# Layer 1's FFN down projection by seven products on 2x2 blocks for 16 of its 22 tiles

## The chip, the cores and the metric

The kernel runs on one core of one Trainium2 chip. TensorE (PE) multiplies, VectorE (DVE) and ScalarE (ACT) do elementwise work, GpSimd (POOL) and SyncE (SP) issue DMAs here. The metric is the device time of one execution in microseconds (us), as the median of several runs. Times of stages come from one profiled execution, counted from its span's start.

## The reference

A two-layer encoder trunk on 1024 tokens of width 1024. Every layer ends with a SwiGLU FFN, whose output is gated and added to the residual stream; a final RMS norm follows layer 1. What the change touches is the product with `w2` in layer 1:

```python
def swiglu(h, w1, w3, w2):
    return (jax.nn.silu(h @ w1) * (h @ w3)) @ w2
...
        h = rms_norm(x, norm_ffn[layer]) * (1.0 + scale_f) + shift_f
        x = x + gate_f * swiglu(h, ffn_w1[layer], ffn_w3[layer], ffn_w2[layer])
    return rms_norm(x, final_norm)
```

`w1` and `w3` are 1024 x 2816, `w2` is 2816 x 1024.

## The kernel before

The activations lie transposed: a tile holds 128 features in the partitions and 1024 tokens, used as two halves of 512 (`HALVES`). The hidden width 2816 makes 22 such tiles, `acts[0]` to `acts[21]`; the model width makes 8 row tiles, `xT[0]` to `xT[7]`.

Each float32 operand of a matmul is split into a high part, rounded to the type fp32r by an ACT copy, and a low part, the rest, by a DVE subtract (`split_into`, L262). A product is then three passes: high times high, high times low, low times high. PE gets one matmul of 128x128 by 128x512 for each pass, each with a weight load of its own.

The FFN (`ffn`, L589) has two stages. In the up products, `w1` and `w3` are taken in 11 pairs of tiles; a pair is two units (one of each weight). From the second pair on, a unit is done by seven products of blocks instead of eight (Winograd's form of Strassen's scheme): the weight blocks and their sums are the left operands, made one by one by `prep` (ACT and DVE) and three products ahead; the activations and their sums are the right operands, `B["11"]`, `B["t1"]` and so on, made once. A product has 12 matmuls (L626 to L628). After the two units of a pair, `done(p, s)` stores the two finished tiles in DRAM (`sp_f`, by POOL), except for the last four, which stay.

The down projection reads the tiles back in groups of 4, 4, 4, 4, 3 and 3, splits them, and adds each group's product with `w2` to the residual `xT` by one DVE operation for each half (`matvec_add`, L795, matmuls at L303, additions at L813). The last group goes one half at a time (`matvec_halves`, L823), so that the final norm (`final`, `normed`, L485) of the first half runs beside the products of the second.

SBUF is cut into equal buffers that the code calls pages, `repage(nf, nr)`: nf of float32 and nr of fp32r, each handed out first in, first out. PSUM has eight banks. The order of instructions on each engine is set when the kernel is built: a scheduler reorders what the code emits. At run time each engine works its queue in order, and an instruction that waits holds back all behind it.

Of the kernel before, what the change touches and what calls it, by code (L numbers as in the profile page):

```python
# [10 lines left out]
F32 = mybir.dt.float32  # L11
# [10 lines left out]
P = 128  # L22
# [54 lines left out]
class Kern:  # L77
# [407 lines left out]
    def normed(self, xT, steps, use, lag, keep=None):  # L485

        nc = self.nc
        acc, sq = self.page(), [self.page() for _ in range(2)]  # L490
        todo, r = deque(), []

        def some(c):
            for _ in range(min(c, len(todo))):
                use(*todo.popleft())

        def half(n):
            r.append(self.rstd(acc, n))
            todo.extend((n, m, r[n]) for m in range(KT))

        for n, m in steps:
            cs = HALVES[n]
            s = sq[m % 2][:, cs] if m else acc[:, cs]
            nc.scalar.activation(out=s, in_=xT[m][:, cs], func=AF.Square)
            if m:
                nc.vector.tensor_tensor(out=acc[:, cs], in0=acc[:, cs], in1=s, op=ALU.add)
            if keep is not None:
                nc.sync.dma_start(out=keep[m][:, cs], in_=xT[m][:, cs])
            if n == 1:
                if m == lag:  # L510
                    half(0)
                elif m > lag:
                    some(2)
        self.free(sq)
        half(1)
        some(2 * KT)
        self.free(acc)
        self.fbank(r)
# [70 lines left out]
    def ffn(self, xT, before, layer, up=iter(()), down=iter(()), low=None):  # L589
# [86 lines left out]
        acts = {}  # L676

        def done(p, s):
            for a in range(2):
                j = 2 * p + a  # L680
# [5 lines left out]

        done(0, s)
        B["t3"] = B.pop("12")
# [27 lines left out]
        for u in range(2, len(units)):  # L716
# [13 lines left out]
            for name in ("11", "t2", "21", "t1", "t3", "t4", "22"):  # L730
# [5 lines left out]
                if u == len(units) - 1:  # L736
                    self.free(B[name])
                if name == "11":
                    nc.scalar.copy(q, ps)
# [22 lines left out]
            if w is w3:  # L762
                done(p, s)
            run(some(up, 3))
        run(up)


# [24 lines left out]
        at, n = groups[-1]  # L792
        return xT, self.matvec_halves(xT, w2[at * P : (at + n) * P, :], ys, layer, 5, low)

    def matvec_add(self, xT, w, ys, layer, part, g=0, keep=None, low=False):  # L795
# [1308 lines left out]
def build(ctx, tc, ins, out):  # L2104
# [73 lines left out]
    ys = K.hyena(hw_in, h, lambda y: project(xd, y, hw_out[0], 1))  # L2178
    K.repage(13, 33)
    xT = [K.unspill(d) for d in xd]  # L2180
# [86 lines left out]
```

## Time and profile before

| | |
|---|---|
| median of 3 runs | 3352.37 us (3352.03 to 3354.47) |
| profiled execution's own time | 3352.85 us |
| its span | 3351.1 us |
| layer 1's up products | up to some 3083 us |
| layer 1's down projection | 3083 to 3331 us |
| final norm of the second half, transposes, output | 3331 to 3351 us |

Rows of the timeline and of groups read: line, engine, operation, tiles written and read (p is any SBUF buffer, bk a PSUM bank), partitions by elements, count, busy time and mean, and then the idle time just before with what ended it ("<-"). Windows give, for each stretch, the busy time of PE, PEld (weight loads), DVE, ACT and POOL with counts, the clock granted to PE, the mean busy share of the 16 DMA engines, and GB/s.

### The profile page before, as it was taken

Reading aid. Unit: us, or ns where it says so; the run is one execution under the profiler, and the core shown is the slowest. Engines: PE = TensorE matmul, PEld = TensorE weight load, DVE = VectorE, ACT = ScalarE, POOL = GpSimd, SP = SyncE. Lnnn points to the kernel's source line nnn. Section 1 sums busy time; section 2 is a strip of 40 time slices with the busy share of each in tenths; the row PEclk is TensorE's granted clock in tenths of the full one; section 3 lists DMA queues with packets and bytes.
Section 4 is the critical chain, followed back from the end, with each engine's and each line's share of the span. In section 5 each row is a group of like instructions: output and inputs, shape, how many; then the busy total and the mean of one; then the engine's idle time right before and its main releaser. Section 6 shows DMA issues by size and latency. Waiting matters only on the chain.

```text
span 3351.1 us, 50857 instructions
## 1 busy us (share of the span) xinstructions
PE 3143.0 (94%) x20195; PEld 2552.3 (76%) x20195; DVE 2331.4 (70%) x3755; ACT 1231.4 (37%) x2144; POOL 196.9 (6%) x443
## 2 busy tenths in 40 slices
PE   6999999988989989999999999988977899999998
PEld 4787766766767878888888887877866788888887
DVE  6465565665766897887877666698998686666545
ACT  4632365555546442533333333221220443333211
POOL 2000000000001110000001210000000000000000
PEclk8999999989989999999999999999988999999999
DMA  8654433333323235344448983332446322234311
GB/s 281 219 179 142 142 96 71 74 85 72 100 65 113 85 134 201 101 145 145 157 132 291 353 296 133 107 113 89 145 169 226 132 82 76 76 107 144 118 48 51
DMA packets 331375, 460.23 MB, mean 137 GB/s; under 512 B 101816, under 2 KB 233745, under 8 KB 331136
## 3 DMA queue, kind: packets, MB, share of 16 engines
q1 hardware_dynamic: 292576, 322.04, 31.2%
q0 software_dynamic: 38384, 134.86, 11.4%
q8 instruction: 159, 2.61, 0.3%
q14 instruction: 80, 0.66, 0.1%
q10 hardware_dynamic: 176, 0.07, 0.0%
HBM read 312.71 MB, written 141.56 MB: 136 GB/s over the span
## 4 chain that ended last, share of the span: by engine, by line
PE 73%; DVE 11%; DMA 8%; ACT 3%; issue 3%; SPq 1%; POOL 0%; DVEq 0%; ACTq 0%; POOLq 0%
PE bk L303 27%; PE bk L626 8%; PE bk L628 8%; PE bk L627 8%; PE bk L1840 2%; DVE p L1722 2%; PE bk L1374 2%; PE bk L1310 2%; PE bk L996 1%; PE bk L975 1%; PE bk L1859 1%; DMA p<-in_mix_w_in_dram 1%; DVE p L264 1%; PE bk L952 1%; DMA p<-in_ada_w_dram 1%
## 5 line engine op out<-in xcount | busy, mean ns | idle before, releaser
L303 PE MATMUL bk<-p,p 128*128 128x512 f32 x5136 | 1228.0, 398 | 73.0 <-ACT p L263 43.2
L303 PEld LDWEIGHTS bk<-p,p 128*128 128x128 f32 x5136 | 974.7, 191 | 289.2 <-ACT p L263 45.6
L263 ACT ACTIVATE p<-p 128x512 fp32r<-128x512 f32 (+3 forms) x542 | 403.1, 759 | 937.5 <-PE bk L627 292.3
L264 DVE TENSOR_TENSOR p<-p,p 128x512 fp32r<-128x512 f32 (+3 forms) x542 | 452.1, 850 | 237.4 <-ACT p L263 195.6
L627 PE MATMUL bk<-p,p 128*128 128x512 f32 x1248 | 485.5, 389 | 3.8 <-DVE p L264 3.8
L626 PE MATMUL bk<-p,p 128*128 128x512 f32 x1248 | 485.0, 390 | 0.0
L628 PE MATMUL bk<-p,p 128*128 128x512 f32 x1248 | 484.7, 389 | 0.2 <-DVE p L264 0.2
L627 PEld LDWEIGHTS bk<-p,p 128*128 128x128 f32 x1248 | 234.3, 188 | 53.1 <-DVE p L264 4.7
L628 PEld LDWEIGHTS bk<-p,p 128*128 128x128 f32 x1248 | 234.3, 188 | 49.2 <-DVE p L264 0.6
L626 PEld LDWEIGHTS bk<-p,p 128*128 128x128 f32 x1248 | 234.3, 188 | 48.1
L813 DVE SCALAR_TENSOR_TENSOR p<-bk,mod,p 128x512 f32<-128x512 f32 x192 | 135.0, 746 | 84.7 <-PE bk L303 83.9
L1722 DVE TENSOR_TENSOR p<-p 128x512 f32<-128x512 f32 x240 | 152.9, 692 | 0.4
L455 DVE SCALAR_TENSOR_TENSOR p<-p,cond,p 128x512 f32<-128x512 f32 x140 | 104.6, 749 | 47.7 <-DMA p<-in_ada_w_dram 45.8
L1840 PE MATMUL bk<-p,p 128*128 128x256 f32 x512 | 125.7, 393 | 6.5 <-DVE p L1761 2.3
L956 DVE TENSOR_REDUCE mx<-bk 128x1 f32<-128x512 f32 x128 | 86.6, 686 | 39.1 <-PE bk L953 37.7
L1840 PEld LDWEIGHTS bk<-p,p 128*128 128x128 f32 x512 | 95.1, 193 | 22.4 <-DVE p L1761 3.1
L1068 ACT COPY p<-bk 128x512 f32<-128x512 f32 (+1 forms) x80 | 43.4, 589 | 177.7 <-PE bk L303 70.6
L960 ACT ACTIVATE p<-bk,mx 128x512 f32<-128x512 f32 x128 | 87.2, 688 | 46.4 <-DVE mx L957 42.5
L976 ACT COPY p<-bk 128x512 f32<-128x512 f32 x128 | 73.5, 588 | 77.3 <-PE bk L975 74.6
L1374 PE MATMUL bk<-p,p 64*64 64x64 f32 x2048 | 86.3, 232 | 13.0 <-DMA p<-o 10.4
L1374 PEld LDWEIGHTS bk<-p,p 64*64 64x64 f32 x2048 | 75.4, 144 | 29.2 <-issue 13.5
L975 PE MATMUL bk<-k_ident,p 128*128 128x128 f32 x512 | 88.6, 302 | 8.2 <-ACT p L976 4.7
(408 smaller groups left out, 4134.7 us busy)
## 6 DMA issues: line engine op xcount, KB each, us to landing
p<-in_ffn_w_dram SPq DMA_DIRECT2D x120, 512.0 KB, 4.7
p<-in_ada_w_dram SPq DMA_DIRECT2D x96, 512.0 KB, 4.5
sp_f<-p POOLq DMA_DIRECT2D x36, 512.0 KB, 5.5
p<-sp_f POOLq DMA_DIRECT2D x36, 512.0 KB, 5.8
hs<-p POOLq DMA_DIRECT2D x32, 512.0 KB, 3.1
p<-hs SPq DMA_DIRECT2D x32, 512.0 KB, 4.5
p<-sp_r SPq DMA_DIRECT2D x24, 512.0 KB, 6.3
p<-sp_x SPq DMA_DIRECT2D x24, 512.0 KB, 4.4
```

Source lines behind the costliest of these rows:

```text
L263: self.nc.scalar.activation(out=hi, in_=src, func=AF.Copy)
L264: self.nc.vector.tensor_tensor(out=lo, in0=src, in1=hi.bitcast(F32), op=ALU.subtract)
L303: nc.tensor.matmul(ps[n], a, b[:, HALVES[n]], start=s, stop=e)
L455: nc.vector.scalar_tensor_tensor(out=acc, in0=wt[:, i], scalar=self.cond[:, k : k + 1], in1=acc, op0=ALU.mult, op1=ALU.add)
L626: nc.tensor.matmul(ps, op[:, 0, k], mh, start=start and k == 0, stop=False)
L627: nc.tensor.matmul(ps, op[:, 0, k], ml, start=False, stop=False)
L628: nc.tensor.matmul(ps, op[:, 1, k], mh, start=False, stop=stop and k == 3)
L813: nc.vector.scalar_tensor_tensor(out=xs, in0=ps[n], scalar=self.modc(layer, part, m), in1=xs, op0=ALU.mult, op1=ALU.add)
L975: nc.tensor.transpose(pt[:, j], pr[:, k * P : (k + 1) * P], self.ident)
L1374: nc.tensor.matmul(pt[H[p], pr], lhs(e, pr, p), rhs[H[p], 8 * e + pr], start=True, stop=True)
L1722: tt = lambda o, a, b, op: nc.vector.tensor_tensor(out=o, in0=a, in1=b, op=op)
L1840: nc.tensor.matmul(ps[j][:, ri], F[2 * d + t2 // 4][:, t2 % 4, 128 * ri : 128 * ri + 128], tp[:, j, d], start=d == 0, stop=d == 1)
```

## The change

For the pairs 0 to 7 of layer 1, the two finished tiles are no longer stored as they are. They are taken as the four blocks of a right operand of seven products: two tiles by two halves. `done` becomes a generator with seven steps; one step is emitted after each product of the next pair. A step makes one right operand: ACT writes its high part (`hi`) and the negated high part (`neg`), POOL stores `hi` in DRAM, SP stores the float32 value, and a POOL DMA with `accum_op=ALU.add` adds `neg` to that in DRAM, so the low part is made there. Four of the steps make the next sum in place by a DVE subtract.

The down projection of layer 1 is a new function, `ffn_down`. Six tiles (18 to 21, 16, 17) go as before. The other sixteen go in two groups of eight: in a group, for each of four blocks of rows (c) there are seven products, each over four k's of 128. The left operands are blocks of `w2` and their sums (`lefts`), the right ones are read back by POOL (`rights`), two names ahead. What a product gives is added to up to four blocks of `xT`. For layer 0 `done` does what it did, one product later. The fp32r buffers of this stage go from 33 to 35, and `normed` counts the tiles of each half itself, since they now come in another order.

```diff
--- before.py
+++ after.py
...
         for n, m in steps:
             cs = HALVES[n]
-            s = sq[m % 2][:, cs] if m else acc[:, cs]
+            i = seen[n]
+            seen[n] += 1
+            s = sq[i % 2][:, cs] if i else acc[:, cs]
             nc.scalar.activation(out=s, in_=xT[m][:, cs], func=AF.Square)
-            if m:
+            if i:
...
-                if m == lag:
+                if i == lag:
                     half(0)
-                elif m > lag:
+                elif i > lag:
...
+        yd = {}
         def done(p, s):
+            if layer and p < 8:
+                b11, b12, b21, b22 = (s[b][:, HALVES[n]] for b in range(2) for n in range(2))
+                for name, src, out, x, y in (
+                    ("11", b11, None, None, None),
+                    ("22", b22, None, None, None),
+                    ("21", b21, b11, b12, b11),
+                    ("t1", b11, b12, b22, b12),
+                    ("t3", b12, b22, b22, b11),
+                    ("t2", b22, b21, b21, b22),
+                    ("t4", b21, None, None, None),
+                ):
+                    d, dl = yd[p, name] = [self.dp.tile([P, 512], dt, tag=f"yd{p}{name}{i}", name=f"yd{p}{name}{i}") for i, dt in enumerate((F32R, F32))]
+                    op = self.page((P, 2, 512), F32R)
+                    hi, neg = op[:, 0], op[:, 1]
+                    nc.scalar.activation(out=hi, in_=src, func=AF.Copy)
+                    nc.scalar.activation(out=neg, in_=hi.bitcast(F32), func=AF.Copy, scale=-1.0)
+                    nc.gpsimd.dma_start(out=d, in_=hi)
+                    nc.sync.dma_start(out=dl, in_=src)
+                    nc.gpsimd.dma_start(out=dl, in_=neg.bitcast(F32), accum_op=ALU.add)
+                    self.free(op)
+                    if out is not None:
+                        tt(out=out, in0=x, in1=y, op=S)
+                    yield
+                self.free(s)
+                return
...
-        done(0, s)
+        side = done(0, s)
...
+                run(some(side, 1))
...
             if w is w3:
-                done(p, s)
+                run(side)
+                side = done(p, s)
             run(some(up, 3))
+        run(side)
         run(up)
+        if layer:
+            return self.ffn_down(xd, acts, yd, w2)
...
+    def ffn_down(self, xd, acts, yd, w2):
...
+        self.repage(25, 23)
+        ys = [self.split(acts[j] if j > 17 else self.unspill(acts[j], nc.gpsimd)) for j in (18, 19, 20, 21, 16, 17)]
+        load = lambda mp: [self.load_w(w2[at * P : (at + n) * P, mp * 256 : mp * 256 + 256], n, 256) for at, n in ((18, 4), (16, 2))]
...
+            for m in (2 * mp, 2 * mp + 1):
+                cs = slice((m % 2) * P, (m % 2) * P + P)
+                xT.append(self.unspill(xd[m]))
+                ps = [self.bank() for _ in range(2)]
+                self.mm3(ps, [(hi[:, k, cs], lo[:, k, cs]) for hi, lo in wt for k in range(hi.shape[1])], ys)
+                for n in range(2):
+                    stt(xT[m][:, HALVES[n]], m, ps[n])
+                self.fbank(ps)
...
+        def rights(g, name):
+            out = [self.page((P, 2, 512), F32R) for _ in range(4)]
+            for k, t in enumerate(out):
+                for i in range(2):
+                    nc.gpsimd.dma_start(out=t[:, i], in_=yd[4 * g + k, name][i])
+            return out
+        names = ("11", "21", "t2", "t3", "t4", "t1", "22")
+        order = [(name, c) for name in names[:5] for c in range(4)]
+        order += [(names[5 + (i > 0 and i % 2 == 0 or i == 7)], c) for i, c in enumerate((0, 1, 0, 2, 1, 3, 2, 3))]
+        def lefts(g):
+            s3 = []
+            for name, c in order:
+                (a11, a21), (a12, a22) = [[raws[g, c, b][:, :, a * P : a * P + P] for a in range(2)] for b in range(2)]
+                if name == "t2":
+                    if c % 2 == 0:
+                        s3.append(self.page((P, 2, 4, P)))
+                    tt(out=s3[c // 2][:, c % 2], in0=a11, in1=a21, op=ALU.subtract)
+                    tt(out=a21, in0=a21, in1=a22, op=ALU.add)
+                    tt(out=a11, in0=a21, in1=a11, op=ALU.subtract)
+                elif name == "t4":
+                    tt(out=a12, in0=a12, in1=a11, op=ALU.subtract)
+                src = {"11": a11, "21": a12, "t2": a11, "t4": a22, "t1": a21, "22": a12}.get(name)
+                op = self.page((P, 2, 4, P), F32R)
+                self.split_into(op[:, 0], op[:, 1], s3[c // 2][:, c % 2] if src is None else src)
...
+            ops = deque(next(left) for _ in range(3))
...
+            for g in range(2):
+                ts = [self.page((P, 2, 512)) for _ in range(4)]
+                for i, (name, c) in enumerate(order):
+                    if i % 4 == 0:
+                        fetch()
+                    ops.extend(itertools.islice(left, 2 if g and i > 11 else 1))
+                    ps = self.bank()
+                    op = ops.popleft()
+                    for k, t in enumerate(R[g, name]):
+                        nc.tensor.matmul(ps, op[:, 0, k], t[:, 0], start=k == 0, stop=False)
+                        nc.tensor.matmul(ps, op[:, 0, k], t[:, 1], start=False, stop=False)
+                        nc.tensor.matmul(ps, op[:, 1, k], t[:, 0], start=False, stop=k == 3)
+                    self.free(op)
...
+                    m = 2 * c
+                    c11, c21, c12, c22 = ((m + a, n) for n in range(2) for a in range(2))
+                    add = lambda at, src: stt(xT[at[0]][:, HALVES[at[1]]], at[0], src)
+                    end = None
+                    if name == "11":
+                        nc.scalar.copy(U2, ps)
+                        add(c11, ps)
+                    elif name == "21":
+                        end = c11
+                    elif name == "t2":
+                        tt(out=U2, in0=U2, in1=ps, op=ALU.add)
+                    elif name == "t3":
+                        tt(out=U3, in0=U2, in1=ps, op=ALU.add)
+                        add(c21, U3)
+                        add(c12, U2)
+                    elif name == "t4":
+                        end = c21
+                    elif name == "t1":
+                        end = c22
+                        add(c22, U3)
+                        add(c12, ps)
+                    else:
+                        end = c12
+                    if end is not None:
+                        add(end, ps)
+                    self.fbank(ps)
+                    if name == "t1" and c == 3:
+                        self.free(ts)
+                    if g and end is not None:
+                        yield end[::-1]
+        for b in range(2):
+            loads(0, b)
+        return xT, steps()
...
-    K.repage(13, 33)
+    K.repage(13, 35)
...
```

How instructions move, at three places. First ACT, in the up products, within one pair. In the rows, L263 (L264 after) is the high part of a split, L726 (L758) a silu and L739 (L772) a PSUM copy of the unit; names are buffers, and the last number tells them apart. Before:

```order
L726 ACTIVATE p_114<-p_94 128x512
L263 ACTIVATE p_10872<-p_122 128x512
L726 ACTIVATE p_114<-p_94 128x512
L263 ACTIVATE p_242<-p_122 128x512
L726 ACTIVATE p_130<-p_102 128x512
L263 ACTIVATE p_10636<-p_118 128x512
L739 COPY p_110<-bk_64 128x512
L263 ACTIVATE p_10672<-p_122 128x512
L263 ACTIVATE p_10660<-p_126 128x512
L263 ACTIVATE p_10872<-p_102 128x512
```

After, at such a place, with the steps' copies L700 (`hi`) and L701 (`neg`) in the buffers 10636 and 10872:

```order
L700 ACTIVATE p_10636<-p_122 128x512
L701 ACTIVATE p_10636<-p_10636 128x512
L264 ACTIVATE p_242<-p_94 128x512
L700 ACTIVATE p_10636<-p_106 128x512
L700 ACTIVATE p_10872<-p_106 128x512
L701 ACTIVATE p_10636<-p_10636 128x512
L701 ACTIVATE p_10872<-p_10872 128x512
L264 ACTIVATE p_18885<-p_118 128x512
L772 COPY p_130<-bk_69 128x512
L700 ACTIVATE p_10636<-p_122 128x512
L264 ACTIVATE p_18889<-p_94 128x512
L700 ACTIVATE p_10872<-p_122 128x512
```

Between the splits for the next products there now stand the copies of the steps, and the second copy into 10636 comes three rows behind the first.

Second POOL, in the same stage. Before, two stores for each pair:

```order
L213 DMA sp_f_20720<-p_110 128x1024
L213 DMA sp_f_20718<-p_122 128x1024
L213 DMA sp_f_20956<-p_114 128x1024
L213 DMA sp_f_20954<-p_130 128x1024
L213 DMA sp_f_21192<-p_122 128x1024
```

After, twelve of the fourteen of one pair, L702 storing `hi` and L704 adding `neg`:

```order
L702 DMA yd_20745<-p_10872 128x512
L702 DMA yd_20723<-p_10636 128x512
L704 DMA yd_20746<-p_10872 128x512
L704 DMA yd_20724<-p_10636 128x512
L702 DMA yd4t_20794<-p_10872 128x512
L702 DMA yd4t_20770<-p_10636 128x512
L704 DMA yd4t_20795<-p_10872 128x512
L704 DMA yd4t_20771<-p_10636 128x512
L702 DMA yd4t_20846<-p_10872 128x512
L702 DMA yd4t_20822<-p_10636 128x512
L704 DMA yd4t_20847<-p_10872 128x512
L704 DMA yd4t_20823<-p_10636 128x512
```

The stores of a pair go from two of 512 KB to fourteen of 256 KB on POOL, which use two buffers in turn, each store that adds behind the plain ones.

Third DVE, in the last products. L840 (L839 after) adds a PSUM bank to the residual, L506 (L509) sums squares for the final norm, and the two rstd rows belong to the norm of the first half. Before:

```order
L840 SCALAR_TENSOR_TENSOR p_110<-bk_66,mod,p_110 128x512
L840 SCALAR_TENSOR_TENSOR p_82<-bk_64,mod,p_82 128x512
L506 TENSOR_TENSOR p_86<-p_86,p_102 128x512
L840 SCALAR_TENSOR_TENSOR p_98<-bk_69,mod,p_98 128x512
L524 TENSOR_SCALAR rstd_587<-bk_70 128x4
L506 TENSOR_TENSOR p_86<-p_86,p_114 128x512
L528 RECIPROCAL rstd_587<-rstd_587 128x4
L840 SCALAR_TENSOR_TENSOR p_94<-bk_65,mod,p_94 128x512
```

After:

```order
L839 SCALAR_TENSOR_TENSOR p_110<-bk_66,mod,p_110 128x512
L839 SCALAR_TENSOR_TENSOR p_106<-bk_66,mod,p_106 128x512
L839 SCALAR_TENSOR_TENSOR p_22301<-bk_64,mod,p_22301 128x512
L839 SCALAR_TENSOR_TENSOR p_22305<-bk_64,mod,p_22305 128x512
L509 TENSOR_TENSOR p_118<-p_118,p_86 128x512
L839 SCALAR_TENSOR_TENSOR p_110<-bk_69,mod,p_110 128x512
L527 TENSOR_SCALAR rstd_587<-bk_70 128x4
L509 TENSOR_TENSOR p_118<-p_118,p_130 128x512
L531 RECIPROCAL rstd_587<-rstd_587 128x4
L839 SCALAR_TENSOR_TENSOR p_22317<-bk_65,mod,p_22317 128x512
```

A bank of the product t1 is now added to two blocks of the residual, where each bank was added to one.

More of the change, by code (lines that the diff above doesn't have):

```diff
@@ L1 @@
+import itertools
 import math
@@ L490, in normed @@
         acc, sq = self.page(), [self.page() for _ in range(2)]
-        todo, r = deque(), []
+        todo, r, seen = deque(), [], [0, 0]
         def some(c):
```

40 lines of the change are left out of this document (added).

## Prediction

> **What bounds the kernel now.** First the page: PE is the busiest engine, and the chain that ended last runs on it for 73% of the span.
>
> ```profile
> PE 3143.0 (94%) x20195; PEld 2552.3 (76%) x20195; DVE 2331.4 (70%) x3755; ACT 1231.4 (37%) x2144; POOL 196.9 (6%) x443
> ...
> PE 73%; DVE 11%; DMA 8%; ACT 3%; issue 3%; SPq 1%; POOL 0%; DVEq 0%; ACTq 0%; POOLq 0%
> ```
>
> Such shares are averages over many stages, so next comes the view by stretches, cut at this change's stages: layer 1's up products (2700 to 3083), its down projection (3083 to 3331), the end, and, for comparison, 200 us of layer 0's down projection.
>
> ```profile
> 2700.00:3083.00 383.00, 383.00 (x1691) 317.16 (x1690) 265.07 (x410) 129.14 (x207) 11.17 (x21) 1.00 0.27 91
> 3083.00:3331.00 248.00, 246.75 (x1108) 203.62 (x1106) 127.82 (x165) 51.21 (x59) 7.91 (x15) 1.00 0.25 80
> 3331.00:3351.10 20.10, 9.00 (x48) 7.67 (x48) 10.31 (x18) 3.93 (x8) 0.00 (x0) 0.70 0.42 168
> 1800.00:2000.00 200.00, 198.81 (x876) 164.02 (x875) 131.84 (x150) 69.34 (x69) 41.46 (x78) 1.00 1.03 350
> ```
>
> The columns are PE, PEld, DVE, ACT and POOL busy with counts, then the granted clock, the DMA share and GB/s. In both stages PE is busy all the time at clock 1.00, with DVE at 69% and 52% and ACT at 34% and 21%. PE is the bound, so fewer matmuls mean less time, as long as every other engine keeps up. Whether busy means full, the view of groups in the down projection and six rows of the timeline say:
>
> ```profile
> L303 PE MATMUL bk<-p,p 128*128 128x512 f32 x1056 | 240.4, 389 | 0.0
> ...
> 2845.07 0.39 PE L627 MATMUL bk<-p,p 128*128 128x512 f32 x1
> 2845.29 0.39 PE L628 MATMUL bk<-p,p 128*128 128x512 f32 x1
> 2845.52 0.39 PE L626 MATMUL bk<-p,p 128*128 128x512 f32 x1
> 2845.74 0.39 PE L627 MATMUL bk<-p,p 128*128 128x512 f32 x1
> 2845.97 0.39 PE L628 MATMUL bk<-p,p 128*128 128x512 f32 x1
> 2846.20 0.39 PE L626 MATMUL bk<-p,p 128*128 128x512 f32 x1
> ```
>
> A matmul is listed with 389 ns, but matmuls start every (2846.20 - 2845.07)/5 = 0.226 us, and 383 us hold 1691 of them, 0.2265 each. The pitch is the price, not the mean duration. A product of 12 matmuls takes 2.71 us.
>
> **What is removed.** The down projection has 22 x 8 x 3 x 2 = 1056 matmuls (tiles, row tiles, passes, halves), the count in the row above. Afterwards six tiles go as before, 6 x 8 x 6 = 288, and sixteen by 2 groups x 28 products x 12 = 672. Removed: 96 matmuls, 96 x 0.226 = **21.7 us**, all on the path. The new products change the stationary operand at each matmul like L626 to L628 do, and those hold the same pitch, so I price them alike.
>
> The Trainium skill, "TensorE: Matmul & The Clock Gate", section "Wait — 56ns, not 53.3ns?", gives 215.7 ns from start to start for 512 columns on a warm array. By that figure the term would be 20.7 us; the trace has 226 ns, and the trace decides.
>
> **What is added beside the up products.** For eight pairs of up tiles there are seven steps, one after each product: two ACT copies (L700, L701), one SP store and two POOL stores of 256 KB, the second adding to what SP stored, and in four steps a DVE subtract (L707). Prices:
>
> ```profile
> L263 ACT ACTIVATE p<-p 128x512 fp32r<-128x512 f32 x140 | 88.4, 632 | 224.6 <-PE bk L627 164.8 <-DVE p L706 22.4 <-DVE p L751 16.3
> ...
> 3003.32 0.68 DVE L750 TENSOR_TENSOR p<-p,bk 128x512 f32<-128x512 f32 x1
> 3003.92 0.68 DVE L751 TENSOR_TENSOR p<-p,bk 128x512 f32<-128x512 f32 x1
> ...
> 3320.84 5.36 DVE L2087 SCALAR_TENSOR_TENSOR p<-p,cols,bk 128x512 f32<-128x512 f32 x8
> ```
>
> ACT gets 112 x 0.632 = 71 us, 129 + 71 = 200 of 383. DVE works at a pitch of 0.60 us, so 32 subtracts are 19 us, 265 + 19 = 284 of 383. As work both lie beside PE and cost nothing. If ACT's slack were gone, each added copy would cost 0.63. The same edit lets layer 0 issue its two stores of a pair one product later; POOL is 6% busy, so I put nothing on that, nor on the counter in the norm, which adds no instruction.
>
> **The wait that is added.** It is on ACT: the negated copy goes into an SBUF page that the step before, or two before, handed to the accumulating store, and must wait for its landing. Queued behind it on ACT are the operand splits for the coming products, and PE waits for those. In the changed order the SBUF pages of a pair form a chain: four accumulating stores (names 11, 21, t1, t2) follow each other on one SBUF page, and then it serves an operand. Each link is one copy (0.63), about 0.1 for the signals, and the landing time T. Against it stands PE's lead: seven operands stand between the first copy and the operand that reuses that SBUF page, and four more are ready, since the five operand buffers were always refilled as PE freed them (the idle time of L263 above is 164.8 us "<-PE bk L627"). That is 11 x 2.71 = 29.8 us. So 4 x (T + 0.73) must stay under 29.8: PE stalls once **T is over about 6.7 us**, by 4 x (T - 6.7) for each of eight pairs, 32 us for each us of T.
>
> The trace has no accumulating DMA. The nearest rows are the landing times of SP's 256 KB stores (sp_r, at the start of this FFN), of POOL's 512 KB stores (sp_f, in the up products), and of POOL's loads where the DMA engines are full (1800 to 2000):
>
> ```profile
> DMA to landing us min/median/max: 2.0/2.1/6.3
> ...
> DMA to landing us min/median/max: 2.9/5.4/7.6
> ...
> p<-sp_f POOLq DMA_DIRECT2D x17, 512.0 KB, 8.8
> ```
>
> T lies between 2.0 and 8.8. An accumulating store of 256 KB reads two operands, so it moves what a POOL store of 512 KB reads; I take that row, **5.4 us**. It is below 6.7, so the stall is 0; at 8.8 it is 8 x 4 x 2.1 = 67 us.
>
> The Trainium skill, "Collectives: The Full Stack", section "The bandwidth ceiling: the fold count and why AG ≠ RS ≠ AR", says that an add in the DMA engine costs no cycles of its own but a second source read, which halves the rate. Its "DMA: Bandwidth & Descriptors", section "Anatomy of one DMA — SWDGE (gpsimd) path", has a fit of 2.0 us plus bytes over 436 GB/s; an estimate by both pages for 512 KB of reads is 3.2 us, no stall either. No run here shows it yet.
>
> The traffic also matters. At the full rate of 350 GB/s a plain 256 KB takes 0.75 us of all DMA engines, an accumulating one at twice that 1.5: 14 x 0.75 + 7 x 1.5 = 21 us for a pair, on top of 0.27 x 38 = 10, so 31 of the pair's 38 us. It fits, with little room in the half in which the steps run.
>
> **What is added in the second half.** Two groups of 28 products last 56 x 2.71 = 152 us. DVE has 56 splits, 32 sums of left blocks and 16 sums of products at 0.60, and 72 scaled additions at 5.36/8 = 0.67: 62 + 48 = 110 of 152 us, 73%. The thickest places (t1 with three additions and a split, 2.6 us; t3 with a sum, two additions and a split, 2.5) still fit a product, and operands run three products ahead. I cost it at nothing; if the lead were gone, the places over 2.71 (21 while the sums for t2 are made, t3 while those for t4 are) would cost some 0.4 us each, 16 of them, 6 us.
>
> The right operands come back by 8 POOL loads of 256 KB for each name, 2 MB per 10.8 us, 194 GB/s, two names ahead. Before, POOL issues such a DMA in 0.53 us:
>
> ```profile
> 3007.30 0.53 POOL L213 DMA_DIRECT2D sp_f<-p  x1 [35.59 <-DVE p L728]
> ```
>
> Eight issues take 4.2 of 10.8 us. At 1800 to 2000 the DMA engines are full at 350 GB/s, 78 POOL transfers among them, and PE is busy 198.8 of 200 us; 194 is well below. Nothing again, with one exception: the second name's loads take SBUF pages that the direct tiles free at their end, so 4.2 + 5.4 = 9.6 us must fit the first name's 10.8. I allow **2 us** for this start and the turn between groups; the bounds are 0 and, were two loads to land at the full engines' 8.8, 2 x (4.2 + 8.8 - 10.8) = 4.
>
> At the change of the SBUF pages' numbers the six tiles are split on ACT and DVE while PE has 43 matmuls of ready tiles (43 x 0.226 = 9.7 us); the last tile needs three DVE operations and an ACT copy (1.06 for 1024 columns), under 5 us. Nothing.
>
> **The end.** Now PE ends its last product at 3330.4, and the rest hangs on DVE:
>
> ```profile
> 3328.11 2.33 PE L303 MATMUL bk<-p,p 128*128 128x512 f32 x9
> 3332.77 1.05 PE L476 MATMUL bk<-k_ones,p 128*128 128x1 f32 x8 [2.32 <-DVE p L506]
> ...
> 3330.49 0.75 DVE L840 SCALAR_TENSOR_TENSOR p<-bk,mod,p 128x512 f32<-128x512 f32 x1 [1.23 <-PE bk L303]
> ```
>
> DVE has 1.23 us to spare ahead of the last addition. Afterwards the last eight products carry 16 additions in place of 8 (+5.4 us of DVE) in 8 x (2.71 - 2.03) = 5.4 us more time, and the last two products carry one each. It comes out even; I allow **1 us**, bounds 0 and 4.
>
> **The sum**, against the profiled execution's own 3352.85 (span 3351.1, 1.75 around it): -21.7 + 2 + 1 = -18.7, so 3334.2. The median of the runs shown is 0.5 lower, 3352.37; I give **3334**.
>
> **The rivals.**
>
> *The accumulating store lands late* (ends slower). For it: nothing in the trace shows T, the threshold is only 1.3 us above the row I chose, and the traffic comes in bursts: 21 transfers in seven steps. Against it: these engines carry 27% now. The saving is used up at T = 6.7 + 18.7/32 = 7.3 us; at 8.8 the time is 3334 + 67 = 3401, at 7.6, the longest of the 512 KB stores here, 3334 + 29 = 3363. The Trainium skill, "DMA: Bandwidth & Descriptors", section "Issuing engines are not separate DMA queues", says that DMAs of all issuing engines run on the same 16 engines; by that rule splitting the stores over SP and POOL buys no bandwidth, and this rival is its result here.
>
> *The saving is given back in the up products*, T between 7.1 and 7.5 or the first pair delayed: within 0.2% of before, 3346 to 3359.
>
> *The second half turns to DVE or to the loads*: 6 us of thick places and 4 of late loads, 3334 + 8 = 3342. For it: 73% of DVE with every operand passing through it. Against it: the up products ran at 69% with no idle PE.
>
> *The products are not saved* (the scheduler serialises the stages, and PE waits where groups change): the 96 matmuls are gone by the order of instructions, so only the waits can eat them; this lies in the second rival.
>
> **How the numbers follow.** Forecast, 3329 to 3339: 0.52. Second half, 3339 to 3346: 0.13. Given back, 3346 to 3359: 0.12. Late landing, over 3359: 0.23. Faster by over 0.2% (below 3345.7; 0.2% is about what a measurement of this kernel can tell from no change) is 0.65, the same 0.12, slower 0.23. The range starts at 3329, below the sum with both allowances at 0 (3331), and reaches into the late landing to T of about 8, 3334 + 32 x 1.3 = 3375; beyond it I leave about 0.15. The likeliest sign's own range is 3329 to 3346.
>
> **What would show it.** PE should be busy all through the up products, with L626 to L628's successors at 0.0 idle; if I am wrong there, their rows show idle time released by ACT or DVE, and ACT's L701 idle time "<-DMA yd". The new products' 672 matmuls should start every 0.226 us, with DVE near 73%. The landing times of the accumulating stores should be around 5.4; over 6.7 the forecast falls. Idle PE in the products while waiting for "DMA p<-yd" would speak for the second rival, and more than 21 us from PE's last product to the end for a late DVE.

## The result, and the profile after

| | before | after |
|---|---|---|
| median, us (4 runs each) | 3353.42 (3352.03 to 3355.23) | 3330.61 (3329.36 to 3337.36) |
| ratio, 95% interval | 1 | 0.9938 (0.9923 to 0.9952) |
| profiled execution's own time / span, us | 3352.85 / 3351.1 | 3329.79 / 3328.0 |

The change is faster by 22.8 us; 3334 was forecast. The page of the changed kernel has PE as the bound as before:

```profile
PE 3118.2 (94%) x20099; PEld 2529.8 (76%) x20099; DVE 2371.6 (71%) x3851; ACT 1290.8 (39%) x2288; POOL 319.5 (10%) x635
```

PE has 96 matmuls fewer, POOL's busy time rises by 122.6 us and DVE's by 40. To place the gain, the two stages are cut at PE's own rows. Timeline of before, the first up product of layer 1, the first matmul of the down projection and the last ones:

```profile
2654.94 0.61 PE L626 MATMUL bk<-p,p 128*128 128x512 f32 x2
...
3083.52 46.86 PE L303 MATMUL bk<-p,p 128*128 128x512 f32 x206
...
3329.83 0.61 PE L303 MATMUL bk<-p,p 128*128 128x512 f32 x2
```

The same rows of after, with the first of the seven products (L928) between them:

```profile
2653.77 0.61 PE L629 MATMUL bk<-p,p 128*128 128x512 f32 x2
...
3083.69 46.63 PE L304 MATMUL bk<-p,p 128*128 128x512 f32 x205
...
3148.97 0.39 PE L928 MATMUL bk<-p,p 128*128 128x512 f32 x1
...
3307.07 0.39 PE L930 MATMUL bk<-p,p 128*128 128x512 f32 x1
```

Start to start, the up products took 428.6 us before and 429.9 after; from there to the end of the last product it was 246.9 and 223.8. Both stages together: 675.5 and 653.7, **21.8 us less**. The rest of the span's 23.1 is 1.2 us ahead of these stages and 0.1 behind them. The 1.2 is no effect that I can name: in the profiles of the experiments, where the earlier stages are the same, the first up product starts anywhere between 2643.6 and 2667.9. From here on I therefore compare these two stages and not spans. They repeat to a few tenths of a microsecond, but for one stall in the first pair that comes up below.

Windows of after at these cuts (columns as in the prediction):

```profile
2653.80:3083.70 429.90, 427.02 (x1890) 352.90 (x1889) 324.53 (x511) 216.88 (x376) 82.83 (x117) 1.00 0.68 172
3083.70:3149.00 65.30, 65.30 (x290) 54.07 (x289) 29.76 (x44) 9.46 (x13) 11.37 (x22) 1.00 0.51 162
3149.00:3307.50 158.50, 158.45 (x721) 131.13 (x719) 118.58 (x185) 47.65 (x78) 47.35 (x90) 1.00 0.65 190
3307.50:3328.00 20.50, 8.85 (x48) 7.45 (x48) 9.62 (x17) 2.98 (x6) 0.00 (x0) 0.76 0.41 162
```

The six direct tiles and the seven products keep PE busy without a gap; DVE has 75% in the seven products (the first half's norm included), DMA 65%. In the up products 2.9 us are idle, of which 2.0 is the wait at their first product that before has too. The other 0.9 is new, and groups of that stage and the view of the accumulating store's line show where it comes from:

```profile
L629 PE MATMUL bk<-p,p 128*128 128x512 f32 x592 | 229.4, 389 | 0.9 <-ACT p L264 0.9
...
L701 ACT ACTIVATE p<-p 128x512 fp32r<-128x512 f32 x56 | 34.6, 628 | 41.2 <-DMA yd<-p 26.7 <-DMA yd4t<-p 2.4 <-DMA yd1t<-p 2.3
```

```profile
ACT p L701: 40.9, 30
DVE p L265: 13.9, 8
...
DMA to landing us min/median/max: 3.8/4.7/10.5
```

The prediction counted the accumulating store alone. The plain store of `hi` (L702) holds the same SBUF page, and its view says:

```profile
ACT p L700: 21.8, 14
...
DMA to landing us min/median/max: 2.3/5.1/8.8
```

The added wait is there. ACT's L701 waited 41 us for landings, 30 times, and its L700 another 22 us for the plain store's, 14 times. DVE waited 14 us, eight times, before the low part of the operand that takes the page next (L265). These waits reached PE only once, in the first pair (2721.5), for 0.9 us.

### The profile page after: what moved, and what is told of

Same layout as the page of the kernel before. It is cut to its first block, busy times and chain, and to the rows that moved or that the text cites. A ratio compares the mean times of both kernels' runs of the same rounds, so it can differ in the third digit from the quotient of the medians.

```text
span 3328.0 us, 51413 instructions
## 1 busy us (share of the span) xinstructions
PE 3118.2 (94%) x20099; PEld 2529.8 (76%) x20099; DVE 2371.6 (71%) x3851; ACT 1290.8 (39%) x2288; POOL 319.5 (10%) x635
## 5 line engine op out<-in xcount | busy, mean ns | idle before, releaser
L304 PE MATMUL bk<-p,p 128*128 128x512 f32 x4368 | 1057.8, 401 | 70.8 <-ACT p L264 39.5
L304 PEld LDWEIGHTS bk<-p,p 128*128 128x128 f32 x4368 | 832.4, 192 | 260.0 <-ACT p L264 42.3
L264 ACT ACTIVATE p<-p 128x512 fp32r<-128x512 f32 (+3 forms) x566 | 402.2, 727 | 798.5 <-PE bk L630 174.9
L265 DVE TENSOR_TENSOR p<-p,p 128x512 fp32r<-128x512 f32 (+3 forms) x566 | 450.4, 813 | 216.0 <-ACT p L264 180.1
L630 PE MATMUL bk<-p,p 128*128 128x512 f32 x1248 | 485.6, 389 | 3.7 <-DVE p L265 3.7
L629 PE MATMUL bk<-p,p 128*128 128x512 f32 x1248 | 485.1, 390 | 0.9 <-ACT p L264 0.9
L631 PE MATMUL bk<-p,p 128*128 128x512 f32 x1248 | 484.4, 389 | 0.0
L630 PEld LDWEIGHTS bk<-p,p 128*128 128x128 f32 x1248 | 234.3, 188 | 52.4 <-DVE p L265 4.5
L629 PEld LDWEIGHTS bk<-p,p 128*128 128x128 f32 x1248 | 234.3, 188 | 49.7 <-ACT p L264 1.3
L631 PEld LDWEIGHTS bk<-p,p 128*128 128x128 f32 x1248 | 234.2, 188 | 49.2 <-DVE p L265 0.4
L2016 PEld LDWEIGHTS bk<-p,p 128*128 128x128 f32 x512 | 95.4, 194 | 25.4 <-DVE p L1937 4.9
L989 DVE SCALAR_TENSOR_TENSOR p<-bk,mod,p 128x512 f32<-128x512 f32 x112 | 78.7, 746 | 24.6 <-PE bk L304 23.4
```

What stands on the lines that cost most here:

```text
L264: self.nc.scalar.activation(out=hi, in_=src, func=AF.Copy)
L265: self.nc.vector.tensor_tensor(out=lo, in0=src, in1=hi.bitcast(F32), op=ALU.subtract)
L304: nc.tensor.matmul(ps[n], a, b[:, HALVES[n]], start=s, stop=e)
L629: nc.tensor.matmul(ps, op[:, 0, k], mh, start=start and k == 0, stop=False)
L630: nc.tensor.matmul(ps, op[:, 0, k], ml, start=False, stop=False)
L631: nc.tensor.matmul(ps, op[:, 1, k], mh, start=False, stop=stop and k == 3)
```

## The experiments

In all of them the stage behind the up products took what it takes in the changed kernel, 223.7 to 223.8 us, unless said otherwise. "Up" is the time of the up products, cut as above; 428.6 before, 429.9 after. Ratios are against runs of before on the same chip.

| | edit | median, us | ratio, 95% interval | up, us |
|---|---|---|---|---|
| e1 | one SBUF page for a pair's steps | 3376.02 | 1.0070 (1.0052 to 1.0087) | 478.1 |
| e2 | e1, a step each second product | 3352.16 | 1.0014 (0.9996 to 1.0031) | 459.8 |
| e3 | a step each second product | 3332.49 | 0.9938 (0.9917 to 0.9958) | 428.5 |
| e4 | low part by DVE | 3331.29 | 0.9938 (0.9923 to 0.9952) | 428.8 |
| e5 | eight tiles by seven products | 3339.84 | 0.9969 (0.9957 to 0.9981) | 430.1 |
| e6 | steps of pair 0 alone | 3325.64 | 0.9941 (0.9918 to 0.9963) | 433.0 |
| e7 | right operands one name ahead | 3332.50 | 0.9945 (0.9926 to 0.9963) | 430.2 |
| e8 | left operands' low parts twice | 3339.89 | 0.9968 (0.9953 to 0.9982) | 432.4 |
| e9 | two SBUF pages for a pair's steps | 3330.52 | 0.9941 (0.9925 to 0.9958) | 430.1 |
| e10 | 33 fp32r buffers | 3382.23 | 1.0089 (1.0061 to 1.0116) | 487.6 |
| e11 | e1 with the low part by DVE | 3327.22 | 0.9926 (0.9899 to 0.9953) | 428.4 |
| e12 | e3 with the low part by DVE | 3322.26 | 0.9914 (0.9890 to 0.9938) | 428.5 |

### Is the saving the removed matmuls? (e5, e6)

e5: `p < 8` becomes `p < 4`, one group of seven products instead of two, and the six direct tiles become fourteen:

```diff
-            if layer and p < 8:
+            if layer and p < 4:
...
+        groups = [(18, 4), (8, 4), (12, 4), (16, 2)]
...
-            for g in range(2):
+            for g in range(1):
```

> Only pairs 0 to 3 take the steps and only eight tiles go by seven products; the other fourteen go in groups as in the kernel before. Theory A (the removed matmuls are the saving): 48 matmuls less than before, 48 x 0.227 = 10.9 us, ratio to before 0.9967, about 3341 where before is 3352; PE's down projection takes 236 us from its first to its last matmul (246.9 before, 223.8 in the changed kernel). Rival (the change has a cost or gain of its own that does not go with the number of tiles): before less 7 or less 14.

From the first up product to the last product of all it took 664.8 us, against 675.5 before and 653.7 after: 10.7 and 21.8 us saved with 8 and 16 tiles, where 48 and 96 matmuls of 0.2266 us are 10.9 and 21.8. So the sum goes with the matmuls. By stages it hides two fixed terms that cancel. Up is longer by 1.3 us (1.5 in e5), which is the first pair's stall. The stage behind it is shorter by 23.1 us (12.3 in e5), some 1.4 more than the removed matmuls. In that stage the transposes of the first half's norm wait for DVE before, and take 5.46 us from first to last, where they take 4.05 after. Timelines of before, then of after:

```profile
3322.72 4.18 PE L2095 MATMUL bk<-k_ident,p 128*128 128x128 f32 x28
3327.52 0.66 PE L2095 MATMUL bk<-k_ident,p 128*128 128x128 f32 x4 [0.61 <-DVE p L840]
...
3300.45 4.05 PE L2271 MATMUL bk<-k_ident,p 128*128 128x128 f32 x32
```

e6 leaves out the steps of pairs 1 to 7, and the second half reads pair 0's right operands instead:

```diff
+            if layer and 0 < p < 8:
+                self.free(s)
+                yield
+                return
...
-                    nc.gpsimd.dma_start(out=t[:, i], in_=yd[4 * g + k, name][i])
+                    nc.gpsimd.dma_start(out=t[:, i], in_=yd[0, name][i])
```

> The steps are made for pair 0 alone; pairs 1 to 7 leave them out, and the second half reads pair 0's right operands in the place of theirs (the same loads in number and size). Theory A (the side work is hidden): the up products take 428.6 to 429.9 us from first to last matmul as in before and after, 3328 to 3331. Rival (side work costs PE what no wait shows, by clock or by late splits): the up products more than 1.5 us shorter.

Up is not shorter without seven eighths of the side work. It is 3.1 us longer than after, by one stall of 2.4 us in pair 0 (its steps are still there), where after has 0.9 and e5 and e7 have 1.1 and 1.2. The side work of the other pairs costs PE nothing.

### What keeps the added wait from PE? (e1, e2, e3)

In e1 the page is taken once for a pair, not once for a step:

```diff
+                op = self.page((P, 2, 512), F32R)
...
-                    op = self.page((P, 2, 512), F32R)
...
-                    self.free(op)
...
+                self.free(op)
```

> The seven steps of a pair share one SBUF page, so each negated copy waits for the accumulating store of the step before. Theory A (chain): PE stalls by what the chain of landings on one SBUF page is longer than PE's lead of 29.8 us. With the median landing of the changed kernel, 4.7 us, the chain is 7 x (4.7 + 0.73) = 38.0 us, so 8.2 us for each of eight pairs, 66 us: about 3396 us; were the landings to fall to the 3.8 us that are the shortest seen, 15 us: 3346. ACT's L701 then has over 100 us of idle time and the up products' matmuls idle time released by ACT. Theory B (ACT's waits do not reach PE: operands stand ready for longer than I counted): 3330 to 3334 and no idle time of PE in the up products.

ACT's timeline in one pair of e1 (start, duration, operation, idle time just before it):

```profile
2841.29 0.63 ACT L701 ACTIVATE p<-p 128x512 fp32r<-128x512 f32 x1 [1.15 <-DMA yd<-p]
2841.83 0.62 ACT L264 ACTIVATE p<-p 128x512 fp32r<-128x512 f32 x1
2842.35 0.61 ACT L700 ACTIVATE p<-p 128x512 fp32r<-128x512 f32 x1
2846.29 0.63 ACT L701 ACTIVATE p<-p 128x512 fp32r<-128x512 f32 x1 [3.32 <-DMA yd3t<-p]
2846.82 0.61 ACT L264 ACTIVATE p<-p 128x512 fp32r<-128x512 f32 x1
2847.34 0.61 ACT L700 ACTIVATE p<-p 128x512 fp32r<-128x512 f32 x1
```

L701 waits 3.32 us for the landing of the step before, and the split L264 for a coming product stands behind it. PE's timeline at that place, and then e1's window over all up products:

```profile
2847.49 0.50 PE L629 MATMUL bk<-p,p 128*128 128x512 f32 x1 [1.67 <-ACT p L264]
```

```profile
2646.50:3124.60 478.10, 448.25 (x1889) 356.49 (x1888) 321.58 (x510) 215.28 (x376) 82.28 (x118) 0.98 0.60 154
```

PE is idle 29.9 us, and the clock is 0.98. Up is 48.2 us longer than after. The landings took 4.1 us in the median. Links are 5.0 us (2841.29 to 2846.29), so by the formula of the prediction seven make 35.0, 5.2 over 29.8, or 42 us for eight pairs. Measured are 27 us more of idle PE (29.9 less 2.9) and 48 us more of time, where 66 us were expected from landings of 4.7. Theory A holds in its direction, and its size is of the right order; B falls.

e2 was to show that the pace matters:

```diff
-                run(some(side, 1))
+                if not layer or (u % 2 * 7 + i) % 2 == 0:
+                    run(some(side, 1))
```

> One SBUF page for the seven steps as in e1, but a step after every second product, over both units of a pair. Theory A: the chain of 38.0 us now stands against a pair of 14 x 2.71 = 38 us and the lead of four products, 10.8 us: no stall, 3328 to 3333. Theory C (what matters is the SBUF page taken out of the rotation, not the pace of the chain): the same loss as in e1.

The window of e2 over the up products:

```profile
2650.20:3110.00 459.80, 442.53 (x1889) 354.71 (x1888) 319.35 (x511) 216.19 (x376) 81.76 (x117) 0.99 0.62 160
```

Neither: 29.9 us lost where A had none and C 48. The reason is in ACT's order. Below is one pair, from its first step to its last, in four kernels (H is L700, n is L701, s is a split L264, a point anything else):

```
after  HnsHHnns.HsHns.nHsHnsn
e1     HnsHnsHs.nsHs.nsHnsH.ns.Hsn
e2     HnsHns.HsnHs.nsHnsH.ns.sH.n
e3     HnsssH.nssHn.ssHn.ss.Hn.s.sHnssHn
```

In e2 the scheduler drew the steps together: 8 splits stand between a pair's first and last copies, 9 in e1, and 13 in e3, where the emission is the same as e2's. The negated copies of one pair started from 2779.90 to 2814.11, and in these 34.2 us PE takes 12.6 operands. So e2 didn't do what its edit says, and it doesn't tell A from C. It does show that the lead isn't the 48.8 us of e2's expectation, which counted by the emission. I take it to be the splits that the built order lets past the waits, plus those that stood ready; that is argued, not measured. Why e1, with one split more, lost more than e2 is left open.

e3 is the same edit with the SBUF pages of the changed kernel:

> The changed kernel with a step after every second product, SBUF pages as they were. Theory A: the 0.9 us of idle PE in the up products goes and nothing else changes, 3328 to 3331; ACT's L701 waits under 15 us instead of 41. Theory D (the burst of transfers itself lengthens the up products in a way the waits don't show): over 2 us less than 3330.6.

Its window over the up products, and the row of L701 among the groups of that stage:

```profile
2659.20:3087.70 428.50, 426.50 (x1889) 353.18 (x1888) 320.63 (x511) 222.02 (x376) 81.67 (x117) 1.00 0.67 173
```

```profile
L701 ACT ACTIVATE p<-p 128x512 fp32r<-128x512 f32 x56 | 35.3, 631 | 1.4
```

ACT's L701 waits 1.4 us instead of 41, and up is back at 428.5 (428.6 before): the stall of the first pair is gone, worth 1.4 us. The medians can't tell 1.4 us.

### The chain, the pages or the store? (e9, e10, e4, e11)

e9 sets two pages aside and takes them in turn, so that a chain has four landings as in the changed kernel:

```diff
+                two = [self.page((P, 2, 512), F32R) for _ in range(2)]
...
-                    op = self.page((P, 2, 512), F32R)
+                    op = two[0]
+                    two.reverse()
...
-                    self.free(op)
...
+                self.free(two)
```

> Two SBUF pages set aside for a pair's seven steps, used in turn, a step after each product. Theory A' (the length of the chain on one SBUF page decides: four landings here, seven in e1): no loss, the up products take 428.6 to 431 us, 3328 to 3333. Theory C (setting SBUF pages aside is what cost time in e1 and e2): five buffers are left for the operands, and the up products take 20 us or more longer, 3350 and up.

The window of e9 over the up products:

```profile
2667.90:3098.00 430.10, 427.07 (x1890) 352.93 (x1890) 324.28 (x511) 219.07 (x376) 82.53 (x117) 1.00 0.66 173
```

No loss, so it is not the setting aside: C falls. e10 undoes one number of the change:

```diff
-    K.repage(13, 35)
+    K.repage(13, 33)
```

> The changed kernel with 33 fp32r buffers as before, so operands and steps share five in place of seven. Theory A' : at two buffers in the hands of landing stores, three are left for operands, a lead of two products, 5.4 us, against waits of 4.7 us: stalls in most pairs, 10 to 40 us, 3340 to 3370. Rival (the two further buffers do nothing): 3328 to 3333, no idle PE.

The same window of e10, and L701 among its groups:

```profile
2649.90:3137.50 487.60, 447.79 (x1889) 362.88 (x1888) 319.86 (x511) 217.10 (x375) 81.77 (x117) 0.96 0.59 151
```

```profile
L701 ACT ACTIVATE p<-p 128x512 fp32r<-128x512 f32 x56 | 35.4, 632 | 108.5 <-DMA yd<-p 47.8 <-DMA yd4t<-p 9.6 <-DMA yd0t<-p 9.2
```

Up is 57.7 us longer, PE 39.8 us idle at clock 0.96, and the kernel is slower than before. Landings take 4.0 us in the median, less than in after, but with five buffers for steps and operands L701 waits 108 us for them in place of 41, and few operands stand ready. That few stand ready is concluded from the number of buffers and not measured; the order itself lets 9 to 12 splits past the copies of a pair here, more than the 6 of the changed kernel. The loss is above the 10 to 40 us expected. Without the two further buffers, on which the prediction put nothing, the gain is lost.

e4 leaves out the negated copy, the store of the source and the accumulating store:

```diff
-                    nc.scalar.activation(out=neg, in_=hi.bitcast(F32), func=AF.Copy, scale=-1.0)
+                    tt(out=neg, in0=src, in1=hi.bitcast(F32), op=S)
                     nc.gpsimd.dma_start(out=d, in_=hi)
-                    nc.sync.dma_start(out=dl, in_=src)
-                    nc.gpsimd.dma_start(out=dl, in_=neg.bitcast(F32), accum_op=ALU.add)
+                    nc.gpsimd.dma_start(out=dl, in_=neg)
```

> The low part by a DVE subtract and a plain POOL store; no negated copy, no store of the source, no accumulating store. Theory A: PE stays the bound, 3328 to 3333; DVE in the up products goes from some 285 to 285 + 56 x 0.6 = 319 of 430 us or 74%, ACT falls by 35 us, and the plain stores land in 2 to 5 us. Rival (DVE's burst delays the operands, a step now needs a subtract for itself beside the next sum, 1.2 us more per product in seven products): idle PE released by DVE, 3335 to 3350.

The window of e4:

```profile
2651.60:3080.30 428.70, 426.66 (x1889) 353.05 (x1888) 354.09 (x566) 190.61 (x319) 62.04 (x117) 1.00 0.45 138
```

DVE does 354 of 429 us (83%; the 74% expected started from 285 us of DVE, where after has 325 in this stage), DMA falls from 0.68 to 0.45, and PE is not held up. As fast as the changed kernel, and without the first pair's stall.

e11 is e4's edit on e1: seven landings on one page, but of plain stores.

> One SBUF page for the seven steps as in e1, with the low part by a DVE subtract and plain stores as in e4. A link is now 0.63 + 0.69 + 2.8 of landing and some 0.3 of signals, 4.4 us, and ACT no longer waits between the two copies of a step. Theory L (the accumulating store's landing behind ACT's second copy made e1 slow): 7 x 4.4 = 31 us against 29.8, up to 10 us in all; the up products take 428.6 to 440 us, 3328 to 3341. Theory C: as in e1, 470 us or more.

The landing times of the two plain stores by their lines, high and then low, and the window:

```profile
DMA to landing us min/median/max: 2.3/2.5/6.7
...
DMA to landing us min/median/max: 2.3/2.3/7.1
```

```profile
2652.70:3081.20 428.50, 426.50 (x1890) 353.20 (x1890) 353.93 (x568) 190.80 (x320) 62.76 (x118) 1.00 0.45 138
```

e1's 48 us are gone. With a chain of seven, doing without the accumulating store removes the loss (e11), and with that store, a chain of four removes it (e9). So the loss takes both the chain of seven and what e11 leaves out. That is more than the accumulation: a step of e11 has one copy on ACT in place of two and no store by SP, and the DMA share is 0.45 in place of 0.60. Which of these counts is not shown.

### How near is the second half to its limits? (e7, e8)

e7 asks for the right operands one name ahead (`for _ in range(1)` ahead of the loop, where it was 2):

> The right operands of the second half are asked for one name ahead in place of two. Theory A (eight issues of 0.53 to 0.6 us and a landing of 4.9 us, 9.7 us, fit the 10.8 us of a name): no idle PE in the seven products, 3328 to 3333. Rival (loads are the next bound, since POOL issues later than the name before begins): PE idle on DMA p<-yd at most of the 13 changes of name, 1 to 3 us each, 3345 to 3370.

No wait of PE names yd, and the stage takes 223.8 us as before the edit. The loads have room for this. The edit took less of it than was meant: in the trace, the loads of the second group's first five names still land 18 us ahead of the first product that reads them, where it was 21 to 25 in after. How much room is left beyond that was not tried.

e8 makes every left operand's low part twice:

```diff
+                src = s3[c // 2][:, c % 2] if src is None else src
+                self.split_into(op[:, 0], op[:, 1], src)
+                tt(out=op[:, 1], in0=src, in1=op[:, 0].bitcast(F32), op=ALU.subtract)
```

> Each left operand's low part in the second half is made twice by DVE, 56 more subtracts of 0.6 us. DVE goes from 111 to 145 of 152 us, 95%; the thick places t1 and t3 go from 2.6 to 3.2 us, over a product's 2.71. Theory A (average decides, three operands of lead cover the thick places): idle PE under 5 us, 3330 to 3335. Rival (thick places decide): 16 to 32 places by 0.5 us, 8 to 16 us, and after it a lower granted clock as in the runs with stalls: 3338 to 3350.

Every wait of PE from the first of the seven products to the last, by the timeline:

```profile
3311.59 2.07 PE L483 MATMUL bk<-k_ident,rstd 128*128 128x128 f32 x8 [2.84 <-DVE rstd L531]
3314.51 5.27 PE L2273 MATMUL bk<-k_ident,p 128*128 128x128 f32 x32 [0.84 <-DVE p L2265]
3320.23 0.50 PE L930 MATMUL bk<-p,p 128*128 128x512 f32 x1 [0.46 <-DVE p L2274]
```

The stage is 6.5 us longer (230.3), between the two expectations. No thick place stalls PE; DVE falls behind (100% busy from 3198 to 3218) and the delay comes out in one piece near the end, where the first half's norm needs its sum. So no thick place decides by itself, and DVE had room for some 28 of the 34 us added.

### Both edits together (e12)

> A step after every second product (e3) and the low part by DVE (e4) together. PE stays the bound: the up products take 428.5 us, the down projection 223.8, and ACT waits for no landing: 3326 to 3332, not told from the changed kernel by the medians. Rival (less DMA traffic or fewer waits free something else): under 3325.

From the first up product to the last product it took 652.2 us, 1.5 less than after: 428.5 for the up products and 223.7 behind them, as expected. The median of 3322 lies in the rival's range and looks better than that, but this profile's first up product starts at 2643.6, 10 us earlier than in after, in stages that the edit doesn't touch. What the edit is shown to bring is the 1.5 us. It has the lowest time of the versions.

## Why the prediction was right

- **Removed matmuls, -21.7.** Measured -21.8 over the two stages, and -10.7 with half of them. That the whole comes out this close is partly luck, since the first pair's +1.3 and the transposes' -1.4 cancel (e5). The pitch as the price holds for the new products: 672 matmuls at 0.2269 us on average (3307.46 - 3148.97 less 6.0 us of norm and transposes).
- **Side work, nothing.** Right (e6, e3). DVE's addition in the up products is 324.5 - 304.9 = 20 us (19 predicted), ACT's 216.9 - 160.9 = 56 in place of 71: copies that follow each other start every 0.53 us (2841.29 to 2841.83), not 0.63.
- **The landing time.** 4.7 us in the median, 5.4 predicted, 3.8 to 10.5 in all. The result is under the threshold as forecast. The plain store on the same SBUF page, which the prediction left out, took 5.1. The page estimate of 3.2 us, worked out from the Trainium skill, "DMA: Bandwidth & Descriptors", section "Anatomy of one DMA — SWDGE (gpsimd) path", and "Collectives: The Full Stack", section "The bandwidth ceiling: the fold count and why AG ≠ RS ≠ AR", is below every accumulating store here. At the least these took 3.7 to 4.1 us, where plain ones of the same size from POOL took 2.3 to 2.6. The medians do not rank them: 4.0 to 4.7 for the accumulating ones, and for the plain ones 2.3 to 3.0 in e4 and e11, but 5.1 in after, where the DMA share is 0.68 and not 0.45.
- **The threshold, T over 6.7.** The weak step, though its answer was right. It counted the lead as eleven products. e1 came out in the formula's order of size, e2 far from what it was to give; the lead seems to depend on how many splits the scheduler leaves between the steps (6 in the changed kernel, so by estimate (6 + 4) x 2.71 = 27 us with the four ready ones, and a threshold of 6.0 us by the same formula) and on the buffers (e10). No run here has a median landing over 4.7, so the point itself isn't shown. And the two further buffers were given no price: without them the forecast's sign would have been wrong (e10).
- **The first pair.** Named in the second rival, without a price: its order differs from that of the later pairs, and it cost 0.9 to 2.4 us of idle PE in the kernels that keep a step after each product, 1.4 us of time in after.
- **Second half, +2, and end, +1.** Both 0, and the transposes gave 1.4 us more. The tail is 20.5 us (20.7 before), PE waited for no right operand, and e8 gives DVE's room.
- **The rivals.** The late landing, at 0.23 the largest, did not come. Its mechanism, waits for landings that outlast PE's lead, is real: e1 and e10 bring it about with landings that are not late (4.1 and 4.0 us), by a longer chain and by fewer buffers, and lose 48 and 58 us of the up products, where the rival's times meant 29 to 67 over the forecast. What kept it away here is the chain of four and the buffers. The turn to DVE needs 28 us more of DVE's work, the turn to the loads was not met even with one name ahead (e7).

The 4.4 us between the forecast and the profiled execution's 3329.79 are the two allowances (3), 1.2 from before these stages, and 0.2 of rounding and tail.

## What to carry to other kernels

When a change puts a wait on an engine that also feeds the bound one, read the built order: count the operands that pass between the waits and those that the buffers can hold ready, and multiply by the time of a product, as an estimate; how the code emits the steps does not settle it. Count buffers as part of the price: two SBUF pages made the difference between 0.6% faster and 0.9% slower. And price a hidden load by its margin as well: DVE at 75% was some 28 us of work from mattering.

## What the runs showed of the hardware

A short stall of PE costs more than its length, in two ways. The matmuls behind it start late at first, even at full clock. Timeline of PE in after, at the first pair's stall, where the granted clock stays 1.00:

```profile
2721.52 0.50 PE L629 MATMUL bk<-p,p 128*128 128x512 f32 x1 [0.88 <-ACT p L264]
2721.86 0.40 PE L630 MATMUL bk<-p,p 128*128 128x512 f32 x1
2722.25 0.50 PE L631 MATMUL bk<-p,p 128*128 128x512 f32 x1
2722.58 0.39 PE L629 MATMUL bk<-p,p 128*128 128x512 f32 x1
```

The three starts behind the first are 0.34, 0.39 and 0.33 us apart, 0.4 us more in all than three of 0.2266. Second, the clock can drop. Timeline of PE in e2, some rows left out:

```profile
2802.65 0.39 PE L631 MATMUL bk<-p,p 128*128 128x512 f32 x1
2805.18 0.50 PE L629 MATMUL bk<-p,p 128*128 128x512 f32 x1 [2.14 <-ACT p L264]
...
2806.93 0.63 PE L630 MATMUL bk<-p,p 128*128 128x512 f32 x1
2807.36 0.63 PE L631 MATMUL bk<-p,p 128*128 128x512 f32 x1
...
2809.36 0.40 PE L630 MATMUL bk<-p,p 128*128 128x512 f32 x1
2809.59 0.40 PE L631 MATMUL bk<-p,p 128*128 128x512 f32 x1
```

After 2.14 us of idle time, matmuls start every 0.43 us for some 3 us, and then every 0.23 again; the granted clock from 2805 to 2810 was 0.66, so 1.7 of these 5 us were lost. There are four such stretches in e2's up products (5 us from 2805, 2853, 2904 and 2983, each at 0.66), 6.8 us in all. Up lost 29.9 us in e2 against after: 14.4 are more idle time (17.3 against 2.9), 6.8 the clock, and the 8.7 left over I put down to late starts behind some ten stalls. The length of a gap alone does not decide on the clock: in e1 a gap of 1.59 us (2807.8) was followed by a drop (0.73 from 2807 to 2812), and one of 1.92 us (2734.8) was not (1.00 from 2734 to 2739). The Trainium skill, "TensorE: Matmul & The Clock Gate", section "What's actually happening", puts the drop to half clock after an idle window of about 3.4 us; the pitch agrees with half the clock, but here a gap of 2.1 us was enough.

An accumulating DMA also costs POOL more to issue: 0.88 us in the median in after and 0.86 in e1, against 0.53 for a plain one of the same size in e4 and 0.56 in after.
